# Storing the first tile of a rotary-embedding kernel in two halves, with its rows 4 to 6 computed another way

## The chip, the cores and the metric

The kernel runs on one core of a Trainium2 chip. The metric is the device time of one execution in microseconds (us); smaller is better. Times before the change: 162.01, 161.99 and 161.97 us, median 161.99 us.

## The reference

```python
# x: (16, 512, 1024) float32; cos, sin: (512, 32) float32; 16 heads of 64
x = x.reshape(16, 512, 16, 64)
x1, x2 = x[..., :32], x[..., 32:]
out = concatenate([x1 * cos - x2 * sin, x1 * sin + x2 * cos], axis=-1)
```

The angle depends on the position in the sequence alone and is the same for all heads. In all, 33.55 MB are read and 33.55 MB are written.

## The kernel before

**Tiles and rows.** The 8192 sequence positions are cut into 8 tiles of 8 rows (`TILES`, L33). A "row" here is one position on each of the 128 partitions, 1024 numbers wide, so there are 64 rows, numbered u = 0 to 63; tile t holds rows 8t to 8t + 7. A tile is 4 MB (4096 KB in the profile), 32 KB on each partition. Each entry of `TILES` gives the number of rows, its place in the ring, the pieces in which it is loaded, the pieces in which it is stored, and the numbers of the stores that have to be complete before it may be loaded. Rows are computed in place: the result of a row goes back into the row's own slot of `x_sb`, a ring of 40 rows (`RING`, L43), which is five tiles. So the first five tiles are loaded at once, and tiles 5, 6 and 7 reuse the places of tiles 0, 1 and 2 once those are stored. Tile 0 is loaded in two halves, tile 7 is stored in two halves, and all the rest moves as whole tiles: nine loads of x and nine stores.

**The work of one row.** Each row takes three steps.

1. The cosine product `x * cos`, written to one of three buffers in PSUM (`t1_ps`, `NT1 = 3`). VectorE does it, in `mul` (L322, instruction L346).
2. The sine product, of x with its halves swapped and a sine table that has the signs in it, written to one of six buffers in SBUF (`t2_sb`, `NT2 = 6`). GpSimd does it, in `on_gpsimd` (L267). Where `TWO` (L74) marks a row, one instruction makes the product of that row and the next (L299, 2048 elements per partition); otherwise one instruction makes one row (L295, 1024 elements). Row 3 of each tile (`V_ROWS`, L65) is VectorE's (L334).
3. The sum of the two, back into `x_sb`. There are two ways. For most rows VectorE adds (`comb`, L353, instruction L356). For the rows marked in `PE2` (L68), that is rows 1, 3 and 5 of a tile (from row 2 on and below row 52), TensorE adds the sine product onto the cosine product in PSUM by four multiplications with the identity (L257), and ScalarE copies the result into `x_sb` (L219).

VectorE's order is written out at the end of `on_vector` (L363): `mul(u)`, then `comb(u - 1)` where that row is VectorE's. `mul(u)` waits until the buffer of row u - 3 has been emptied, by VectorE's sum or by ScalarE's copy.

**The queues.** All loads are issued from ScalarE's queue (`on_scalar`, L197): the first six at the start (two halves of tile 0, then tiles 1 to 4) together with the two small tables, and the three late ones behind fixed rows of ScalarE's own loop, by `BEHIND` (L45): tile 5 behind row 23, tile 6 behind row 33, tile 7 behind row 41. Ahead of each, ScalarE waits for the stores that the tile's entry names. All stores are issued from SyncE's queue (`on_sync`, L186), in order. Each waits (`wait_added`, L164) until all rows up to a given one have been summed, by whichever way; that row is the last row of the piece, except for the first store, which is held back by one row more (`HOLD`, L84).

Of the kernel before, what the change touches and what calls it, by code (L numbers as in the profile page):

```python
# [6 lines left out]
def bass_split_heads_rope_kernel(  # L7
# [14 lines left out]
    R1 = seq // P  # L22
# [8 lines left out]


    TILES = (  # L33
        (8, 0, (4, 4), (8,), ()),
        (8, 8, (8,), (8,), ()),
        (8, 16, (8,), (8,), ()),
        (8, 24, (8,), (8,), ()),
        (8, 32, (8,), (8,), ()),
        (8, 0, (8,), (8,), (0,)),
        (8, 8, (8,), (8,), (1,)),  # L40
        (8, 16, (8,), (4, 4), (2,)),
    )
    RING = 40  # L43

# [2 lines left out]
    NU = sum(t[0] for t in TILES)  # L47
# [3 lines left out]
    rows = [(t, r) for t in range(NT) for r in range(TILES[t][0])]  # L51
# [13 lines left out]
    V_ROWS = {8: (3,)}  # L65
    V2 = [r in V_ROWS[TILES[t][0]] for t, r in rows]

    PE2 = [2 <= u < NU - 2 * R1 - 4 and u % 8 in (1, 3, 5) for u in range(NU)]  # L68

    def count(flags):  # L70
        return [sum(flags[: u + 1]) for u in range(NU)]


    TWO = [r in (0, 4, 6) for t, r in rows]  # L74
    n_pool = count([not V2[u] and not (u and TWO[u - 1]) for u in range(NU)])
    n_pe = count(PE2)
    n_comb = count([not a for a in PE2])

# [2 lines left out]
    BANK = 512  # L81
    EH = H * HD // BANK
    LEAD = 1
    HOLD = 1  # L84

    with ExitStack() as stack:
        x_sb = stack.enter_context(nc.sbuf_tensor([P, RING, H, 2, HALF], fp32))
# [55 lines left out]
        def in_dram(flat, t, o, m):  # L143
            n = TILES[t][0]
            run = flat[first_row[t] * P:(first_row[t] + n) * P, :].rearrange("(p r) d -> p (r d)", r=n)
            return run[:, o * dim:(o + m) * dim]
# [5 lines left out]
        def in_sbuf(t, o, m):  # L152
            k = TILES[t][1] + o
            return x_sb[:, k:k + m].rearrange("p n h t d -> p (n h t d)")
# [9 lines left out]
        def wait_added(eng, u):  # L164
            if n_pe[u]:
                eng.wait_ge(sem_a, n_pe[u])
            if n_comb[u]:
                eng.wait_ge(sem_v, n_comb[u])

        def wait_t2_free(eng, u):  # L170
            if u >= NT2:
                v = u - NT2
                if PE2[v]:
                    eng.wait_ge(sem_e, n_pe[v])
                else:
                    eng.wait_ge(sem_v, n_comb[v])
# [5 lines left out]
        def wait_landed(eng, t, r):  # L182
            if (t, r) in load_at:
                eng.wait_ge(sem_in[load_at[t, r]], 16)

        def on_sync(sp):  # L186
            for u in range(NU):
                if u not in store_after:
                    continue
                k = store_after[u]  # L190
                t, o, m = stores[k]

                wait_added(sp, u + HOLD if k == 0 else u)
                sp.dma_start(in_dram(of, t, o, m), in_sbuf(t, o, m)).then_inc(sem_out.get(k, sem_rest), 16)
            sp.wait_ge(sem_rest, 16 * (len(stores) - len(awaited)))

        def on_scalar(ae):  # L197
# [18 lines left out]
            for u in range(NU):  # L216
                if PE2[u]:
                    ae.wait_ge(sem_e, n_pe[u])
# [7 lines left out]
        def on_tensor(pe):  # L226
# [22 lines left out]
            for u in range(NU):  # L249
                if not PE2[u]:  # L250
                    continue
# [15 lines left out]
        def on_gpsimd(pl):  # L267
# [12 lines left out]
            for u in range(NU):  # L280
                t, r = rows[u]
                n = TILES[t][0]
                wait_landed(pl, t, r)
                if V2[u] or (u and TWO[u - 1]):
                    continue
                if n not in seen:
                    seen.add(n)
                    pl.wait_ge(sem_s, SIZES.index(n) + 1)
                m = 2 if TWO[u] else 1
                for v in range(u, u + m):  # L290
                    if v == u + m - 1 or PE2[v - NT2] != PE2[v + 1 - NT2]:
                        wait_t2_free(pl, v)
# [15 lines left out]
        def on_vector(ve):  # L308
# [54 lines left out]
            for u in range(NU + LEAD):  # L363
                if u < NU:
                    mul(u)
                if u >= LEAD and not PE2[u - LEAD]:
                    comb(u - LEAD)

        on_sync(nc.sync)
        on_scalar(nc.scalar)  # L370
        on_gpsimd(nc.gpsimd)
# [35 lines left out]
```

## Time and profile before

| | us |
|---|---|
| median of three runs | 161.99 |
| the profiled execution | 161.94 |
| its span, first to last instruction | 160.5 |
| outside the span (161.94 - 160.5) | 1.44 |

| engine | busy us | share of the span |
|---|---|---|
| VectorE (DVE) | 133.9 | 83% |
| GpSimd (POOL) | 127.0 | 79% |
| TensorE (PE) | 62.5 | 39% |
| ScalarE (ACT) | 21.8 | 14% |

The DMA moved 67.25 MB, 419 GB/s over the span. The page gives busy shares for the whole span and in 40 slices. The last of the profile's parts used here is the trace's list of DMA packets, with start, duration, size and queue of each: queue q10 is ScalarE's (the loads), q1 is SyncE's (the stores). Each piece is cut into 128 packets, one for each partition, eight for each of 16 DMA engines: 32 KB each for a piece of eight rows, 16 KB each for one of four.

The moments of the transfers in the profiled execution, in us from the start of the span:

| transfer | issued | first packet | landed |
|---|---|---|---|
| load of tile 4 | 4.28 | 46.98 | 66.55 |
| load of tile 5 | 60.69 | 66.34 | 85.90 |
| load of tile 6 | 86.67 | 90.27 | 110.86 |
| load of tile 7 | 103.02 | 109.72 | 130.32 |
| store of tile 0 | 35.56 | 39.90 | 60.60 |
| store of tile 1 | 49.65 | 59.27 | 79.95 |
| store of tile 2 | 65.47 | 78.64 | 94.50 |
| store of tile 7, first half | 144.22 | 148.87 | 155.61 |
| store of tile 7, second half | 152.13 | 153.78 | 160.45 |

### The profile page before, as it was taken

What the parts mean: (1) busy time and instruction counts of PE and PEld (TensorE: products, weight loads), DVE (VectorE), ACT (ScalarE), POOL (GpSimd) and SP (SyncE); (2) the same over time, 40 slices, a digit from 0 to 9 for tenths busy, and PEclk for the clock granted to TensorE, in tenths of its full rate; (3) what the DMA queues carried; (4) which work ended last, traced back from release to release, by engine and by line L of the source; (5) the groups of instructions that cost most, each with busy time, mean ns of one, the idle gap of its engine ahead of it and who ended that gap; (6) DMA issues with size and microseconds to landing.
All of it is one profiled execution on the core that took longest, in us unless ns stands there. A gap on an engine that the chain in (4) does not pass through costs nothing.

```text
span 160.5 us, 488 instructions
## 1 busy us (share of the span) xinstructions
PE 62.5 (39%) x90; PEld 22.0 (14%) x90; DVE 133.9 (83%) x120; ACT 21.8 (14%) x23; POOL 127.0 (79%) x38
## 2 busy tenths in 40 slices
PE   6050039048923761489038922893174000000000
PEld 1040023022302220223022301230121000000000
DVE  0023898999899999999999899999999977999800
ACT  0410002202220222022202220213022000000000
POOL 1009999999999999999998999883999559994000
PEclk9999999965585799557965597559569655555555
DMA  5999999999999999999999999999999999999995
GB/s 155 419 439 457 433 482 392 392 515 351 433 392 466 449 392 459 449 400 408 498 400 400 506 392 408 490 408 408 425 466 400 433 457 417 417 449 441 392 421 249
DMA packets 2882, 67.25 MB, mean 419 GB/s; under 512 B 321, under 2 KB 577, under 8 KB 577
## 3 DMA queue, kind: packets, MB, share of 16 engines
q10 hardware_dynamic: 1584, 33.69, 49.8%
q1 hardware_dynamic: 1296, 33.56, 48.5%
q14 instruction: 2, 0.01, 0.0%
HBM read 33.69 MB, written 33.55 MB: 419 GB/s over the span
## 4 chain that ended last, share of the span: by engine, by line
DVE 34%; DMA 21%; issue 15%; PE 13%; POOL 7%; ACT 3%; ACTq 1%; DVEq 0%; POOLq 0%
DMA x_sb<-in_x_dram 17%; DVE x_sb L356 16%; DVE t_ps L346 15%; PE t_ps L257 12%; POOL t_sb L299 6%; DMA stage<-in_sin_dram 4%; DVE t_sb L334 3%; ACT x_sb L219 3%; POOL t_sb L295 1%; PE tab_ps L240 1%; PE t_ps L240 1%; ACTq L203 0%; ACT sine L214 0%; ACTq L180 0%; ACT sine L215 0%
## 5 line engine op out<-in xcount | busy, mean ns | idle before, releaser
L299 POOL TENSOR_TENSOR t_sb<-x_sb,sine 128x2048 f32<-128x2048 f32 x24 | 108.2, 4530 | 18.5 <-ACT sine L215 10.5
L346 DVE TENSOR_TENSOR t_ps<-x_sb,tab_ps 128x1024 f32<-128x1024 f32 x64 | 76.9, 1222 | 13.1 <-PE t_ps L240 9.9
L257 PE MATMUL t_ps<-t_sb,ident 128*128 128x512 f32 x76 | 57.7, 915 | 53.5 <-DVE t_ps L346 47.5
L356 DVE TENSOR_TENSOR x_sb<-t_ps,t_sb 128x1024 f32<-128x1024 f32 x45 | 54.7, 1217 | 4.2 <-POOL t_sb L299 4.1
L257 PEld LDWEIGHTS t_ps<-t_sb,ident 128*128 128x128 f32 x76 | 19.6, 284 | 91.1 <-DVE t_ps L346 74.7
L219 ACT ACTIVATE x_sb<-t_ps 128x1024 f32<-128x1024 f32 x19 | 19.5, 1024 | 92.1 <-PE t_ps L257 92.1
L295 POOL TENSOR_TENSOR t_sb<-x_sb,sine 128x1024 f32<-128x1024 f32 x8 | 18.9, 2359 | 0.0
L334 DVE TENSOR_TENSOR t_sb<-x_sb,tab_ps 128x1024 f32<-128x1024 f32 x8 | 9.7, 1212 | 0.0
L230 PE MATMUL t_ps<-zero 128*128 128x512 bf16 x6 | 2.7, 627 | 1.3 <-DVE zero L309 1.3
L240 PE MATMUL tab_ps<-stage,chosen 128*128 128x128 f32 x4 | 1.2, 453 | 5.0 <-DMA stage<-in_sin_dram 5.0
L207 ACT ACT_TABLE_LOAD x1 | 1.3, 1283 | 4.8 <-issue 4.8
L240 PEld LDWEIGHTS tab_ps<-stage,chosen 128*128 128x128 f32 x4 | 0.9, 321 | 5.8 <-issue 5.8
L240 PE MATMUL t_ps<-stage,chosen 128*128 128x128 f32 x4 | 1.1, 421 | 0.0
L230 PEld LDWEIGHTS t_ps<-zero 128*128 128x128 bf16 x6 | 0.7, 135 | 2.4 <-DVE zero L309 1.2
L309 DVE MEMSET zero<- 128x256 uint32 x1 | 0.3, 272 | 0.9 <-PEq L389 0.9
L214 ACT ACTIVATE sine<-t_ps 128x256 f32<-128x256 f32 x1 | 0.4, 384 | 4.5 <-PE t_ps L240 4.5
L240 PEld LDWEIGHTS t_ps<-stage,chosen 128*128 128x128 f32 x4 | 1.0, 333 | 0.0
L268 POOL MEMSET ident<- 128x128 f32 x1 | 0.2, 206 | 0.3 <-POOLq L389 0.3
L207 ACT ACTIVATE chosen<-ident 128x256 f32<-128x256 f32 x1 | 0.4, 429 | 0.0
L215 ACT ACTIVATE sine<-t_ps 128x256 f32<-128x256 f32 x1 | 0.4, 378 | 0.0
L270 POOL TENSOR_SCALAR_AFFINE_SELECT ident<-ident 128x128 f32<-128x128 f32 x1 | 0.3, 295 | 0.1
L389 POOL MEMSET const-float32-0.0<- 128x1 f32 x1 | 0.1, 99 | 0.3 <-issue 0.3
(5 smaller groups left out, 0.7 us busy)
## 6 DMA issues: line engine op xcount, KB each, us to landing
x_sb<-in_x_dram ACTq DMA_DIRECT2D x7, 4096.0 KB, 27.3
out_dram<-x_sb SPq DMA_DIRECT2D x7, 4096.0 KB, 29.0
x_sb<-in_x_dram ACTq DMA_DIRECT2D x2, 2048.0 KB, 9.4
out_dram<-x_sb SPq DMA_DIRECT2D x2, 2048.0 KB, 9.9
stage<-in_cos_dram ACTq DMA_DIRECT2D x1, 64.0 KB, 7.3
stage<-in_sin_dram ACTq DMA_DIRECT2D x1, 64.0 KB, 7.0
```

The costliest lines, as they stand in the source:

```text
L207: ae.activation(pick[n][:], ident[:].rearrange("q (s k) -> q k s", k=m)[:, :, None, :].broadcast_to([P, m, m, P // m]), COPY,).then_inc(se ...
L214: ae.activation(s_sb[n][:, :, 0, :], raw_sin[n], COPY, scale=-1.0)
L215: ae.activation(s_sb[n][:, :, 1, :], raw_sin[n], COPY).then_inc(sem_s, 1)
L219: ae.activation(xs[:, place_of(u), :], t1_ps[:, u % NT1, :], COPY).then_inc(sem_a, 1)
L230: pe.matmul(t1_ps[:, k, b * BANK:(b + 1) * BANK], zero[:, 0:P], zero[:], start=True, stop=True).then_inc(sem_w, 1)
L240: ins = pe.matmul(to[:, k * R1:(k + 1) * R1, :].rearrange("p r d -> p (r d)"), pick[n][:, k].rearrange("q b s -> q (b s)"), stage[:, c, :] ...
L257: ins = pe.matmul(t1_ps[:, u % NT1, b * BANK:(b + 1) * BANK], ident[:], t2[:, b * BANK:(b + 1) * BANK], start=False, stop=True, skip_group ...
L295: pl.tensor_tensor(t2_sb[:, u % NT2, :, :, :], swapped(k), over_heads(s_sb[n][:, r]), mult).then_inc(sem_p, 1)
L299: pl.tensor_tensor(t2_sb[:, u % NT2:u % NT2 + 2].rearrange("p n h t d -> p (n h) t d"), x_sb[:, k:k + 2, :, ::-1, :].rearrange("p n h t d ...
L334: ve.tensor_tensor(t2_sb[:, u % NT2, :, :, :], swapped(k), over_heads(v_ps[n][:, V_ROWS[n].index(r)]), mult,)
L346: ve.tensor_tensor(t1_ps[:, u % NT1, :].rearrange("p (h d) -> p h d", d=HALF), x_sb[:, k, :, :, :].rearrange("p h t d -> p (h t) d"), c_ps ...
L356: ve.tensor_tensor(xs[:, place_of(u), :], t1_ps[:, u % NT1, :], t2_sb[:, u % NT2, :, :, :].rearrange("p h t d -> p (h t d)"), add,).then_i ...
```

## The change

Tile 0 is stored as two pieces of four rows. The first is issued when row 5 has been summed (row 3, the last of the piece, and two more), the second when row 10 has been summed (row 7 and three more). Since there is one store more, the numbers in the last column of `TILES` move: the load of tile 5 waits for both halves of tile 0. In tile 0 alone, the sine products of rows 4 and 5 become two single instructions instead of one for both, row 5 is summed by VectorE instead of TensorE and ScalarE, and row 6 by TensorE and ScalarE instead of VectorE.

```diff
     TILES = (
-        (8, 0, (4, 4), (8,), ()),
+        (8, 0, (4, 4), (4, 4), ()),
...
-        (8, 0, (8,), (8,), (0,)),
-        (8, 8, (8,), (8,), (1,)),
-        (8, 16, (8,), (4, 4), (2,)),
+        (8, 0, (8,), (8,), (0, 1)),
+        (8, 8, (8,), (8,), (2,)),
+        (8, 16, (8,), (4, 4), (3,)),
     )
...
-    PE2 = [2 <= u < NU - 2 * R1 - 4 and u % 8 in (1, 3, 5) for u in range(NU)]
+    PE2 = [2 <= u < NU - 2 * R1 - 4 and u % 8 in ((1, 3, 6) if u < 8 else (1, 3, 5)) for u in range(NU)]
...
-    TWO = [r in (0, 4, 6) for t, r in rows]
+    TWO = [r in (0, 4, 6) and (t, r) != (0, 4) for t, r in rows]
...
-    HOLD = 1
+    HOLD = {0: 2, 1: 3}
...
-                wait_added(sp, u + HOLD if k == 0 else u)
+                wait_added(sp, u + HOLD.get(k, 0))
```

## The prediction

> **What bounds the kernel now.** I read the page's slices first: no engine is full, but the DMA row is.
>
> ```profile
> DMA  5999999999999999999999999999999999999995
> GB/s 155 419 439 457 433 482 392 392 515 351 433 392 466 449 392 459 449 400 408 498 400 400 506 392 408 490 408 408 425 466 400 433 457 417 417 449 441 392 421 249
> ```
>
> Only the first and the last of 40 slices are not full. The queues say what fills it: loads and stores, half each.
>
> ```profile
> q10 hardware_dynamic: 1584, 33.69, 49.8%
> q1 hardware_dynamic: 1296, 33.56, 48.5%
> ```
>
> The two GB/s extremes in the second row are packets counted where they start, so I summed the packet records with each packet spread over its duration. That gives 433 GB/s in nearly every 2 us stretch from 4 to 158 us, for loads alone, stores alone or both, with two holes: 335 GB/s in 38 to 40 us, and 412 GB/s in 112 to 116. The floor follows: 67.25 MB at 433 GB/s are 155.3 us, and the first packet starts at 1.80, so a kernel that keeps this stream full cannot end its packets before 157.1; they end between 158.6 and 160.13. Moving transfers about inside a full stream gains nothing by itself.
>
> Next the chain of work that ended last, to see whether compute could matter too:
>
> ```profile
> 103.01 0.01 ACT x_sb L219
> 103.02 27.31 DMA x_sb<-in_x_dram
> 130.32 0.07 issue
> 130.39 4.52 POOL t_sb L299
> ...
> 149.81 2.25 DVE x_sb L356 x2
> ```
>
> ScalarE's row 41 releases the load of tile 7, this lands at 130.32, and tile 7's eight rows take until 152.06. The waits of SyncE's queue close it:
>
> ```profile
> SPq L168 <- DVE x_sb L356: 148.1, 9, 34.7
> SPq L195 <- DMA out_dram<-x_sb: 8.0, 1, 8.0
> ```
>
> The last store is issued at 152.13 and needs 8 us. Its first packet starts only at 153.78, each engine going on from the half before it without a gap: the DMA still has a backlog when compute is done. Of its 16 landings, 14 lie at 158.91 to 159.53, the two others at 160.15 and 160.45. **The end is one late DMA engine.** Its lateness is old. The packet records show a load packet at 38.24 that took 2.68 us where 1.21 is usual, just ahead of the first store's first packets; the other 15 took 1.47 to 1.85 there. At 62.08 a store packet took 1.56, beside an 8 KB instruction fetch (61.78, 0.31 us), and the second late engine appears in the landings after that.
>
> **The change part by part.** *The sine products.* The pair of rows 4 and 5 took 4.50 us start to start (13.49 / 3, L299); a single one takes 2.31 (16.30 to 18.61, L295). Two are 4.62: GpSimd is 0.12 us later from row 6 on. Rows 4 and 5 would be ready at 20.97 and 23.28 instead of 23.11 both. VectorE's order decides when they are used:
>
> ```profile
> 25.84 1.22 DVE L356 TENSOR_TENSOR x_sb<-t_ps,t_sb 128x1024 f32<-128x1024 f32 x1
> 27.47 2.36 DVE L346 TENSOR_TENSOR t_ps<-x_sb,tab_ps 128x1024 f32<-128x1024 f32 x2 [0.41 <-ACT x_sb L219]
> 29.74 1.22 DVE L356 TENSOR_TENSOR x_sb<-t_ps,t_sb 128x1024 f32<-128x1024 f32 x1
> ```
>
> Row 4 is summed at 25.84, so both cases are early, and row 8's product, at 32.10 + 0.12, is used at 34.26. Cost: nothing, covered by 2 us.
>
> *The sums.* VectorE has as many as before. Its order after 27.47 becomes product 6, sum 5, product 7, product 8, instead of product 6, product 7, sum 6, product 8: with 1.13 us from start to start, row 5 is summed at 28.60 to 29.82, and product 8 still starts at 30.87. New is that product 9 (33.13) needs row 6 from TensorE and ScalarE. TensorE can start at 28.74 (product 6 ends 28.70). Four multiplications took 3.78 us for row 3 (22.59 to 26.37) and 1.98 for row 5 (26.39 to 28.37, at a granted clock of 0.98 in the window 26 to 34). With ScalarE's 1.02 and two handovers of 0.04 row 6 is in place at 31.8 or 33.6: product 9 waits 0 or 0.5 us. I take 0, from the nearer row, whose clock window covers it, with 0.5 as the upper end. Below zero: if the clock stays high until row 11, the wait of 0.41 us (ACT, ahead of product 14) goes, so compute moves by -0.4 to +0.5. The Trainium skill's page "TensorE: Matmul & The Clock Gate", section "Part 1: The HAM clock gate", has the array fall back to half clock after an idle window of about 3.4 us; the gap ahead of row 6 would be 28.74 - 26.37 = 2.37 us, so by it the wait is 0 and the +0.5 case goes.
>
> *The stores.* The first half is issued at 29.82 + 0.08 = 29.9 instead of 35.56, the second behind row 10's sum (38.79 + 1.22) at 40.1. One issue more is 0.33 us on SyncE, which waits 148 us anyway. With the first store's own delay (35.56 to 39.90, 4.34 us) the first packet runs at 34.2. From 40 to 59 us a load packet and a store packet alternate on each engine: the store's 8 packets took 59.07 - 39.90 = 19.2 us, 2.40 each, two times 1.21. Half-tile packets take 0.61, so a round is 1.82 us, loads get two thirds, and the first half needs 8 x 1.82 = 14.6 us, to 48.8; the second follows with no gap, since it is issued at 40.1. Tiles 3 and 4 have about 14.5 load packets per engine left at 34.2, that is 26.4 us, so they are in at about 61 (before: 65). The second half ends at 62 and lands at 62 to 63.6; if shares went by bytes, it would be 34.2 + 4.19 MB / 216 GB/s = 53.6. This new wait gates the load of tile 5, issued at 60.69 before. Behind ScalarE's wait stands its copy of row 25 (70.40), 6.8 us later, so VectorE isn't reached. The load's first packet would start 3.6 us after the issue (as 86.67 to 90.27), at 64.3 to 67.2, against 66.34 before, with stores filling the gap; tile 5 lands at 86.8 at the latest and is first used at 91.27. Tiles 6 and 7 are released by ScalarE's rows 33 and 41 (86.67, 103.02), with 79.95 and 94.50 as the store landings needed, so the order of transfers is the old one from there.
>
> *The bytes.* 256 packets of 16 KB take 0.611 each instead of 128 of 1.213: 256 x 0.611 - 128 x 1.213 = 1.15 us over 16 engines, +0.07 us. The hole at the first store (15 packets lost 0.26 to 0.63, one 1.47) moves to about 33 us; I cost the move at nothing, since loads run alone around it as before. Bounds: it may vanish (-0.45 us mean, -0.92 at the late engine) or come again at the second half (+0.45).
>
> Sum against the profiled execution: 161.94 + 0.07 + 0 = 162.01; the median stands 0.05 above it: **162.05 us**. What compute moves by is hidden: the bulk of the engines has some 0.3 to 0.6 us to spare at the last store (152.13 plus 1.0 to 1.3, as the first load's 0.80 to 1.80 and 2.10, against 153.7), the late engine one more.
>
> **The rivals.** *Slower, the late engine gets later.* The place is the first store's first packet. For: one engine lost 1.47 there, and each engine's fate differs. If the engine that meets the instruction fetch is the one that is late, 160.15 - 159.53 = 0.62 is added: 162.7; if it loses a packet of 1.21 more in the new alternation, 163.2. It decides from a loss over 1.47 + 0.3. 0.16.
>
> *Slower, the second half pays again*: a hole like the first (+0.45, 162.5), up to an issue-to-packet time on idle engines (+1.0, 163.0). Against: the second half is queued 8 us before the first is done, and the last two halves landed 4.84 us apart, 2.10 MB at 433 GB/s, so a queued transfer costs nothing extra. 0.07. The Trainium skill's page "DMA: Bandwidth & Descriptors", section "Anatomy of one DMA — SWDGE (gpsimd) path", puts about 2.0 us of fixed cost on each DMA; by it, unhidden, the time would be 164.0, and the 4.84 us speak against it here.
>
> *Slower, compute*: product 9's 0.5 us passes through rows 33 and 41 to tile 7 and the last store, where it outlives the reserve: 162.4. 0.05.
>
> *Faster, the lateness does not arise.* Loads around the first store are in another phase, and only one engine in 16 was unlucky. If the second late engine stays, the end is 0.30 earlier: 162.05 - 0.30 = 161.75, 0.12. If it goes too, 0.92: 161.15; between these 0.20. Compute allows it, since tile 7's landing was itself late by that engine (129.2 for the others, and VectorE had waited 1.14).
>
> *That nothing hinges on the change*, the forecast, holds the remaining 0.40.
>
> **How the numbers follow.** A difference over 0.2%, 0.32 us, is what a measurement can tell. Same: 0.40 + 0.12 = 0.52. Faster: 0.20. Slower: 0.16 + 0.07 + 0.05 = 0.28. The range from 161.2 to 162.8 leaves out the worst of the late-engine case and a double hole.
>
> **What would show it.** Right: a DMA row of 9s, the first half issued near 29.9 and the second near 40.1, tile 5's load issued at 62 to 64, row 6's copy ended before 33.13, tile 7 landed within 1 us of 130.32, and one or two late landings at the end. Wrong: a slice with the DMA below 9 in the middle, a second group of long packets near 49, VectorE waiting for ScalarE ahead of 33.1, or all 16 last landings together.

## The result and the profile after

The changed kernel took 163.20 us (median of six runs, 162.47 to 163.34) against 161.98: ratio 1.0072, 95% interval 1.0052 to 1.0093. Two later repeats of it gave 1.0100 (1.0083 to 1.0117) and 1.0081 (1.0050 to 1.0111). It is slower, by 1.2 to 1.6 us; the prediction said 162.05, with 162.8 at most. The profiled execution took 163.32 us, 1.38 more than the one before, with a span of 161.8. Runs over 1.5% longer than the fastest of their kernel are left out of all ratios here: three of the eleven of e4 below, one of the twelve of h1 (166.20) and one of the kernel before (164.41).

The page of the changed kernel, slices and queues:

```profile
DMA  5999999989999999999899999999999999999993
GB/s 190 417 422 429 502 405 389 502 377 401 413 454 441 441 401 452 364 494 397 356 437 470 397 437 462 397 462 437 397 462 437 397 462 437 397 462 409 421 425 170
...
q10 hardware_dynamic: 1584, 33.69, 49.4%
q1 hardware_dynamic: 1440, 33.56, 48.4%
```

The row is as full as before. Two slices show an 8 (32 to 36 and 77 to 81 us), and 144 packets more are on the store queue. The chain that ended last, and SyncE's last wait:

```profile
102.03 0.01 ACT x_sb L219
102.04 27.26 DMA x_sb<-in_x_dram
129.30 0.07 issue
129.37 4.52 POOL t_sb L299
...
148.78 2.26 DVE x_sb L356 x2
```

```profile
SPq L195 <- DMA out_dram<-x_sb: 10.3, 1, 10.3
```

Compute is a microsecond **earlier** than before: tile 7 lands at 129.30 (130.32), the last sum ends at 151.04 (152.06). Yet SyncE waits 10.3 us for the last store instead of 8.0. The 16 landings of that store, one for each DMA engine, from the trace:

```
before 158.91 158.94 159.00 159.00 159.07 159.09 159.30 159.32 159.37 159.38 159.46 159.46 159.47 159.53 160.15 160.45
after  159.06 159.08 159.11 159.19 159.21 159.25 159.35 159.37 159.41 159.60 159.97 160.86 161.37 161.50 161.60 161.79
```

The middle of the row is unchanged, 159.35 and 159.39. What moved is its end: one or two late engines became five, and the last is 1.34 us later, nearly the whole difference of the profiled executions (1.38).

Where these five fell behind is in the packet records. Five store packets at 66.33 to 66.87 took 2.1 to 2.5 us instead of 1.21, just ahead of the first packet of tile 5's load (67.23); at 76.15 to 76.90 five load packets took 2.1 to 2.55, and nine more at 78.5 to 78.9 took 0.2 to 0.4 too long. From 64 to 80 us packets took 15.0 us longer than usual in sum, 0.94 us for each of 16 engines; in the profile before nothing there took longer. These are two places, not one. Ahead of the restart of the loads stand 5.4 of the 15.0 us; 9.4 are in load packets from 76 on, where the store queue goes from tile 1's store to tile 2's (no store packet starts between 75.69 and 77.33). The records have no engine numbers, but a packet starts where the one before it on its engine ended; followed in this way, the five long store packets and the five long load packets lie on the same five engines. The DMA view of that window, before and then after:

```profile
DMA packets 247, 7.05 MB, mean 440 GB/s; under 512 B 32, under 2 KB 32, under 8 KB 32
```

```profile
DMA packets 217, 6.59 MB, mean 412 GB/s; under 512 B 16, under 2 KB 16, under 8 KB 16
```

0.46 MB less in the same 16 us are 1.06 us at 433 GB/s (packets are counted where they start, so half a megabyte is also the most that the edges can hide). The view alone does not decide: the repeat e5 below, with the loss, has 7.01 MB in this window, and f3, without it, 6.82. The sum over packets is the better measure. I call the first place, the long store packets just ahead of the restart, the **restart loss** below.

The compute side did what its waits were worked out to do (VectorE, ScalarE, and ScalarE's queue of the changed kernel):

```profile
28.48 1.22 DVE L356 TENSOR_TENSOR x_sb<-t_ps,t_sb 128x1024 f32<-128x1024 f32 x1
29.61 2.35 DVE L346 TENSOR_TENSOR t_ps<-x_sb,tab_ps 128x1024 f32<-128x1024 f32 x2
31.87 1.22 DVE L356 TENSOR_TENSOR x_sb<-t_ps,t_sb 128x1024 f32<-128x1024 f32 x1
33.00 1.22 DVE L346 TENSOR_TENSOR t_ps<-x_sb,tab_ps 128x1024 f32<-128x1024 f32 x1
```

```profile
31.34 1.02 ACT L219 ACTIVATE x_sb<-t_ps 128x1024 f32<-128x1024 f32 x1 [4.04 <-PE t_ps L257]
```

```profile
63.14 0.33 ACTq L180 DMA_DIRECT2D x_sb<-in_x_dram  x1
```

Row 5 is summed at 28.48, row 6 is copied by 32.36, and product 9 starts at 33.00 with no wait. The last line is tile 5's load, issued at 63.14 as soon as the second half has landed (63.06), 2.45 us later than before.

### The profile page after: what moved, and what is told of

Read it like the earlier page. It is cut to its first block, busy times and chain, and to the rows that moved or that the text cites. A ratio compares the mean times of both kernels' runs of the same rounds, so it can differ in the third digit from the quotient of the medians.

```text
span 161.8 us, 493 instructions
## 1 busy us (share of the span) xinstructions
PE 58.9 (36%) x90; PEld 20.4 (13%) x90; DVE 133.7 (83%) x120; ACT 21.8 (13%) x23; POOL 127.1 (79%) x39
## 4 chain that ended last, share of the span: by engine, by line
DVE 36%; DMA 21%; issue 15%; PE 10%; POOL 7%; ACT 2%; ACTq 1%; DVEq 0%; POOLq 0%
DVE x_sb L356 17%; DMA x_sb<-in_x_dram 17%; DVE t_ps L346 16%; PE t_ps L257 9%; POOL t_sb L299 6%; DMA stage<-in_sin_dram 4%; DVE t_sb L334 3%; ACT x_sb L219 2%; POOL t_sb L295 1%; PE tab_ps L240 1%; PE t_ps L240 1%; ACTq L203 0%; ACT sine L214 0%; ACTq L180 0%; ACT sine L215 0%
## 5 line engine op out<-in xcount | busy, mean ns | idle before, releaser
L299 POOL TENSOR_TENSOR t_sb<-x_sb,sine 128x2048 f32<-128x2048 f32 x23 | 103.6, 4520 | 17.4 <-ACT sine L215 10.3
L257 PE MATMUL t_ps<-t_sb,ident 128*128 128x512 f32 x76 | 54.1, 857 | 56.2 <-DVE t_ps L346 50.1
L257 PEld LDWEIGHTS t_ps<-t_sb,ident 128*128 128x128 f32 x76 | 17.9, 261 | 91.9 <-DVE t_ps L346 77.3
L295 POOL TENSOR_TENSOR t_sb<-x_sb,sine 128x1024 f32<-128x1024 f32 x10 | 23.4, 2349 | 0.0
```

The costliest lines, as they stand in the source:

```text
L257: ins = pe.matmul(t1_ps[:, u % NT1, b * BANK:(b + 1) * BANK], ident[:], t2[:, b * BANK:(b + 1) * BANK], start=False, stop=True, skip_group ...
L295: pl.tensor_tensor(t2_sb[:, u % NT2, :, :, :], swapped(k), over_heads(s_sb[n][:, r]), mult).then_inc(sem_p, 1)
L299: pl.tensor_tensor(t2_sb[:, u % NT2:u % NT2 + 2].rearrange("p n h t d -> p (n h) t d"), x_sb[:, k:k + 2, :, ::-1, :].rearrange("p n h t d ...
```

## The experiments

Runs of one and the same kernel differ: the kernel before took 161.2 to 162.5 us in nearly all of its runs beside the experiments, with medians of 161.72 to 161.92. Each ratio is against those on the same chip.

The first theory was the **dry queue**: half-size store packets leave the loads two thirds of the DMA, so these run out at 61.3; the next load waits for the second half, and its restart among stores loses time. The rivals: the compute part; the earlier store; chance.

**e1, the split alone.** `PE2` and `TWO` as before.

```diff
-    PE2 = [... u % 8 in ((1, 3, 6) if u < 8 else (1, 3, 5)) ...]
+    PE2 = [... u % 8 in (1, 3, 5) ...]
-    TWO = [r in (0, 4, 6) and (t, r) != (0, 4) for t, r in rows]
+    TWO = [r in (0, 4, 6) for t, r in rows]
```

> The store in two halves alone: sine products and sums of tile 0 as before. Dry-queue theory (the second half's landing at 63.1 gates tile 5's load at 63.14, loads run out at 61.3, and at the restart near 66.5 five DMA engines lose 1.1 us each, which ends the kernel late): 163.0 to 163.4 us, several last landings over 1 us behind the bulk. Compute theory (rows 4 to 6 make it slower): 162.0.

162.49, ratio 1.0042 (1.0016 to 1.0068). Of ten runs seven lie at 161.83 to 162.53 and three at 163.22 to 163.30. The profiled one (161.83) has no restart loss, but it is the fastest of the ten. So the split costs something by itself, and by the medians less than the change (the two intervals overlap).

**e2, the compute part alone**, in the kernel before: the two lines of e1 the other way round.

> The new sine products and sums of rows 4 to 6 alone, tile 0 stored whole as before. Dry-queue theory: 161.9 to 162.1, one or two late landings at the end as before. Compute theory: 163.0 or more. Chance theory (any shift of timing redraws which DMA engines are late): anywhere between 161.2 and 163.2.

161.99, 1.0012 (0.9991 to 1.0033): not to be told from nothing. The compute theory falls, as far as these rows alone go.

**e3, both halves late.**

```diff
-    HOLD = {0: 2, 1: 3}
+    HOLD = {0: 5, 1: 1}
```

> Both halves issued behind row 8, when the whole store was issued before (about 35.5), the rest as in the changed kernel. By packets of 16 KB the loads still get two thirds and run out at about 58, the second half lands at about 62, and tile 5's load restarts an empty queue near 66. Dry-queue theory: 162.7 to 163.3, late engines from about 66. Early-start theory (it is the earlier first store that costs): 162.0 as before.

162.40, 1.0023 (1.0004 to 1.0042). The loads ran out at 58.3 and restarted at 66.8 as expected, and no packet near 66 was long. The dry queue alone does not make the loss.

**e4, tile 5 in two loads.**

```diff
-        (8, 0, (8,), (8,), (0, 1)),
+        (8, 0, (4, 4), (8,), (0, 1)),
-    BEHIND = {6: 23, 7: 33, 8: 41}
+    BEHIND = {6: 19, 7: 23, 8: 33, 9: 41}
...
-                        for j in TILES[loads[i][0]][4]:
+                        t, o, m = loads[i]
+                        n_in = len(TILES[t][2])
+                        for j in TILES[t][4] if n_in == 1 else (TILES[t][4][o // m],):
```

> The changed kernel with tile 5 loaded in two halves, each behind the store of the half whose place it takes: the first is issued at about 57 behind ScalarE's row 19, so the load queue does not run dry at 61. Dry-queue theory: 162.0 to 162.2, no group of long packets near 66. Early-start theory: 163.2 as the changed kernel.

Median 163.60, ratio 1.0081 (1.0046 to 1.0117), with a wide spread, 161.74 to 166.23. In the profiled execution, the longest of them and one of those left out of the ratio, tile 5's 16 KB load packets took turns with 32 KB store packets: its last ones ran past 92 us, where tile 5's loading had ended at 84.2 before, tile 7's last packet ended at 135.3 instead of 129.9, and the last store was issued only at 158.66. There the loads got the smaller share, which is another cause; whether the usual runs show it too isn't known, so this kernel says nothing on the theory.

**e5, the changed kernel again**, on the chip of e6 to e8.

> The changed kernel once more, beside the next three on the same chip, since the split alone came out 0.57 us over the kernel before there and the whole change 1.2 us elsewhere. If the change is the split and nothing else, 162.4 to 162.6 as the split alone; if the compute part adds to it, 163.0 or more.

163.37, 1.0100 (1.0083 to 1.0117), with the restart loss (four packets over 0.9 us too long near 66).

**e6, a dry restart without a split**: the kernel before, with tile 5's load held to row 23's sum.

```diff
                     if BEHIND[i] == u:
+                        if i == 6:
+                            ae.wait_ge(sem_v, n_comb[23])
```

> The kernel before, with tile 5's load held on ScalarE until VectorE has summed row 23 (about 65.5 instead of 60.7), so that the load queue runs dry at 65 and restarts near 69 among stores; the store of tile 0 is whole. Dry-queue theory: 162.4 to 163.2, long packets near 68. Packet-size theory (16 KB store packets taking turns with 32 KB load packets give the loads two thirds and pull the 16 DMA engines apart): 161.9 as before.

161.80, 1.0005 (0.9984 to 1.0025). The loads ran out at 64.8 and restarted at 69.0, at no cost. With e3, the dry-queue theory in its plain form is down.

**e7, two transfers of 64 partitions each**, 32 KB packets, in the kernel before.

```diff
-                sp.dma_start(in_dram(of, t, o, m), in_sbuf(t, o, m)).then_inc(sem_out.get(k, sem_rest), 16)
+                for h in ((0, 64), (64, 128)) if k == 0 else ((0, 128),):
+                    sp.dma_start(
+                        in_dram(of, t, o, m)[h[0]:h[1], :], in_sbuf(t, o, m)[h[0]:h[1], :]
+                    ).then_inc(sem_out.get(k, sem_rest), 16)
...
-                            ae.wait_ge(sem_out[j], 16)
+                            ae.wait_ge(sem_out[j], 32 if j == 0 else 16)
```

> The kernel before, with tile 0's store in two transfers of 64 partitions each, issued one behind the other behind row 8: two transfers, yet packets of 32 KB. Packet-size and dry-queue theories: 161.9 as before, loads and stores half and half. Theory of a cost for each transfer: 162.4.

166.12, 1.0295 (1.0237 to 1.0354). None of the theories had this. Packets of both queues were long from 44.9 to 65.2, where these pieces ran. A transfer of half the partitions is a thing of its own here, so it prices nothing of the change.

**e8, one store in 16 KB packets**, in the kernel before.

```diff
-                sp.dma_start(in_dram(of, t, o, m), in_sbuf(t, o, m)).then_inc(sem_out.get(k, sem_rest), 16)
+                to, frm = in_dram(of, t, o, m), in_sbuf(t, o, m)
+                if k == 0:
+                    to = to.rearrange("p (a d) -> p a d", a=2)[:, ::-1, :]
+                    frm = frm.rearrange("p (a d) -> p a d", a=2)[:, ::-1, :]
+                sp.dma_start(to, frm).then_inc(sem_out.get(k, sem_rest), 16)
```

> The kernel before, with tile 0's store as one transfer issued behind row 8, cut into 16 KB packets by naming the two halves of each partition in the other order. Packet-size theory: 162.4 as the split ones, loads out at about 58. Theory of a cost for each transfer, or of the earlier start: 161.9.

161.91, 1.0008 (0.9990 to 1.0025), although the loads ran out at 59.2 and restarted at 66.6. Packet size and dry queue together cost nothing measurable.

So neither part of the change was expensive alone, nor the packets. What was left was the **moment**: e1 issues its first half at 29.14, the change at 29.78, since row 5 is summed by VectorE. In the profile after, engines part there: the first half lands at 47.6 to 47.9 on eleven engines and at 48.5 to 49.0 on five. I supposed that the border between two load pieces near 32.2 does it.

**f1, the split alone at the change's moment.**

```diff
                 wait_added(sp, u + HOLD.get(k, 0))
+                if k == 0:
+                    sp.wait_ge(sem_m, 8)
```

> The split alone, with sums and sine products as before, but SyncE waits in addition for product 7, so that the first half is issued at about 29.85 as in the changed kernel, and not at 29.14. Phase theory (0.6 us later, the store's first packets meet the engines at the border of two load pieces near 32.2; some engines take their first store packet one turn later than the others, and lose over 1 us more near 66): 163.2 to 163.4. Compute theory (rows 4 to 6 themselves add 0.9): 162.4 to 162.5 as the split alone.

162.73, 1.0064 (1.0039 to 1.0090), restart loss in the profile. In this profile the moment brings the loss without the compute part. The time lies between the two theories' figures, and its interval overlaps that of e1, so the times alone do not tell the two moments apart.

**f2 and f3, the change with its first half later and earlier**: `HOLD = {0: 3, 1: 3}` and `HOLD = {0: 1, 1: 3}`.

> The changed kernel with the first half held back by three rows instead of two: issued at about 32.4, first packets near 36.3, in the middle of tile 3's load. Phase theory: 162.3 to 162.6. Compute theory, and a plain cost of two halves with early start: 163.2 to 163.4.

> The changed kernel with the first half held back by one row: issued at about 27.4, first packets near 31.4, ahead of the border. Phase theory: 162.3 to 162.6 if 31.4 is clear of the border, else as the change. Compute theory: 163.2 to 163.4. Theory that the earlier the first store, the more is lost: 163.5 or more.

f2, issued at 33.60: 162.20, 1.0025 (1.0006 to 1.0045). f3, issued at 27.44: 162.01, 1.0011 (0.9994 to 1.0029), so no loss that can be measured with an even earlier store. Compute part, split and early start are all in f3: none of them is the cost by being there.

**f4, the change with the restart held to row 23's sum** (the lines of e6).

> The changed kernel, with tile 5's load held on ScalarE until VectorE has summed row 23 (about 65.4 instead of 63.3). If the loss near 66 belongs to the moment of this restart: 162.3 to 162.6, or long packets moved to near 69. If the engines were parted at the first store already and lose at whatever moment the load queue restarts: 163.2 to 163.4, with long packets near 69.

162.69, 1.0080 (1.0048 to 1.0112). The long store packets went along with the restart: six at 68.7 to 69.0, ahead of the load's first packet at 69.19. The loss belongs to the restart, not to its clock time.

**g1, the change a third time; g2, no border; g3, a moment between.** g2 loads tiles 2 and 3 as one transfer; g3 waits for product 8 (`sp.wait_ge(sem_m, 9)`).

```diff
             t, o, m = loads[i]
-            eng.dma_start(in_sbuf(t, o, m), in_dram(xf, t, o, m)).then_inc(sem_in[i], 16)
+            if t == 3:
+                return
+            to, frm = in_sbuf(t, o, m), in_dram(xf, t, o, m)
+            if t == 2:
+                to = x_sb[:, TILES[2][1]:TILES[2][1] + 16].rearrange("p (a n) h t d -> p a (n h t d)", a=2)
+                frm = xf[first_row[2] * P:first_row[4] * P, :].rearrange("(a p r) d -> p a (r d)", a=2, r=8)
+            eng.dma_start(to, frm).then_inc(sem_in[i], 16)
...
-                eng.wait_ge(sem_in[load_at[t, r]], 16)
+                eng.wait_ge(sem_in[load_at[2 if t == 3 else t, r]], 16)
```

> The changed kernel a third time, as the measure for the next three on the same chip: 163.0 to 163.4, long store packets near 66.

> The changed kernel with tiles 2 and 3 loaded as one transfer, so that the border of two load pieces near 32.2, just where the first store packets come in, is gone; the first half is still issued at about 29.8. Border theory (the loss needs the first store to meet a border): 162.0 to 162.5, no long store packets near 66. If only the moment of the issue counts, or the restart of the load queue: 163.0 to 163.4.

> The changed kernel with the first half issued only when product 8 is done, at about 32.15, between the 29.8 of the change and the 33.6 that gave 162.2: its first packets come in near 36, clear of the border at 32.2. Border theory: 162.0 to 162.4. If 33.6 was better for another reason, between 162.4 and 163.4.

g1: 163.24, 1.0081 (1.0050 to 1.0111). The change has now come out slower in all three of its measurements, each time with long packets near 66 in the profile, so chance falls as a rival too. g2: 163.37, 1.0104 (1.0073 to 1.0136), the engines part and lose as in the change. Tile 2's rows now wait for both tiles, and the last store is issued at 153.14 instead of 151.12; the median of its landings is 159.37 all the same. **The border theory is down.** g3, issued at 32.16: 162.47, 1.0049 (1.0030 to 1.0069), without the restart loss; just over the border theory's figure.

**g4, the whole store, held back by two rows, with the restart held.** `HOLD = 2` in the kernel before, and the lines of e6.

> The kernel before with its whole store of tile 0 held back by two rows (issued at about 39.3, which stands to the border of the loads of tiles 3 and 4 at 41.7 as 29.8 stands to 32.2), and tile 5's load held to row 23's sum, so that the load queue restarts empty. If a border at the first store and a restart are enough, with 32 KB packets too: 162.4 to 163.2, long store packets near 69. If it needs the half-size packets or the two pieces: 161.8.

163.17, 1.0092 (1.0071 to 1.0113). A restart loss with no split at all, on all engines (median of the last landings 160.67). The DMA view of 64 to 80 us for it:

```profile
DMA packets 207, 6.26 MB, mean 391 GB/s; under 512 B 16, under 2 KB 16, under 8 KB 16
```

Now what do the kernels with the loss have in common? In each, tile 4's load and the last store of tile 0 land together. Two runs were to break and to make that meeting: **h1** keeps the change's first moment and holds the second half to row 15 (`HOLD = {0: 2, 1: 8}`); **h2** takes f3's first moment and issues the second half later (`HOLD = {0: 1, 1: 5}` and a wait for TensorE's row 13).

> The changed kernel with its first half issued as there (29.8), but the second held back to row 15 (about 49.6), so that the loads run alone from 47.5 to 53: tile 4 lands at about 59.2, the second half still at about 62.3. Theory of the meeting (the loss comes when tile 4's load and tile 0's last store land within half a microsecond of each other, 62.0 and 62.3 in the change, which all nine kernels with a loss or without fit so far): 162.0 to 162.5, no long store packets near 66. Theory of the first moment (29.8 is enough): 163.0 to 163.4.

> The kernel whose first half is issued at 27.4, which took 162.01 (tile 4 in at 64.9, second half at 60.1), with the second half issued at about 44.9 instead of 40.5, so that both land near 62.2 to 62.9. Theory of the meeting: 162.8 to 163.4, long store packets near 66. Theory of the first moment: 161.9 to 162.2.

h1: 162.25, 1.0031 (1.0011 to 1.0052), eleven runs from 161.60 to 163.00 and one at 166.20, no long packet near 66:

```profile
DMA packets 238, 7.27 MB, mean 455 GB/s; under 512 B 16, under 2 KB 16, under 8 KB 16
```

The first moment is not enough. h2: 162.03, 1.0019 (1.0001 to 1.0038), where the theory of the meeting had 162.8 to 163.4. Its profile has no long packet either, though the two landed 0.2 us apart; but this execution (161.63) is the fastest of the twelve, and two others took 162.81 and 162.86. In most runs, then, the meeting is not enough by itself.

All of these side by side (e4 and e7, with causes of their own, left out); moments from the profiled executions, "in" is the median of the 16 landings, and the two columns of packets give the us in sum by which packets started in that window took longer than usual (1.21 us for 32 KB, 0.61 for 16 KB):

| kernel | first store issued | tile 4 in | tile 0's last store in | store packets, 64 to 72 | load packets, 72 to 82 | ratio |
|---|---|---|---|---|---|---|
| before | 35.56 | 65.82 | 58.53 | 0.0 | 0.0 | 1 |
| e2 compute alone | 35.61 | 65.97 | 58.66 | 0.0 | 0.0 | 1.0012 |
| e6 late restart | 35.49 | 65.73 | 58.48 | 0.1 | 1.4 | 1.0005 |
| f3 earlier | 27.44 | 64.86 | 60.10 | 0.0 | 0.0 | 1.0011 |
| e8 16 KB packets | 35.51 | 59.42 | 62.40 | 0.0 | 2.8 | 1.0008 |
| e3 halves late | 35.50 | 59.16 | 62.17 | 0.0 | 0.0 | 1.0023 |
| f2 later | 33.60 | 59.89 | 62.31 | 0.0 | 10.3 | 1.0025 |
| h1 second half late | 29.73 | 59.05 | 62.15 | 0.0 | 0.2 | 1.0031 |
| g3 between | 32.16 | 60.87 | 62.27 | 0.3 | 2.0 | 1.0049 |
| h2 made to meet | 27.34 | 62.58 | 62.78 | 0.0 | 0.0 | 1.0019 |
| e1 split alone | 29.14 | 61.97 | 62.16 | 0.0 | 0.6 | 1.0042 |
| f1 split, at 29.9 | 29.92 | 61.81 | 62.24 | 4.0 | 12.6 | 1.0064 |
| f4 change, late restart | 29.85 | 62.11 | 62.31 | 5.8 | 8.3 | 1.0080 |
| the change | 29.78 | 62.02 | 62.27 | 5.4 | 9.4 | 1.0072 |
| e5 the change | 29.75 | 62.08 | 62.34 | 5.1 | 1.2 | 1.0100 |
| g1 the change | 29.70 | 62.07 | 62.33 | 6.9 | 4.9 | 1.0081 |
| g2 no border | 29.67 | 62.11 | 62.35 | 9.4 | 6.5 | 1.0104 |
| g4 whole, late | 39.05 | 62.03 | 62.22 | 7.8 | 13.3 | 1.0092 |

**What is shown:** of these, seven kernels have a restart loss in their profile, 4.0 us or more in the store packets of 64 to 72 us, and all others 0.3 or less. Each of the seven costs at least 0.6%, every other one less than 0.5%, though neighbours' intervals overlap and each kernel has one profile. The loss comes just ahead of the restart of the load queue and moves with it (f4); all seven profiles with it have the two landings within 0.5 us; and in h1, with the meeting taken away, it is gone. To take it away h1 issues the second half 10 us later, so the meeting is not the only thing that differs.

**What is argued only:** how much of the time is the restart loss and how much the second place. For the restart speaks e5, with 5.1 us there, 1.2 at the second place and the ratio 1.0100. But f2's profiled execution, the longest of its twelve (162.84), lost 10.3 us in load packets at the second place, with nothing at the restart and the landings 2.4 us apart. So the second place may have a price of its own, and the meeting is no condition for it.

**What stays open:** why some engines lose a packet's time there, and why h2, and most runs of e1, meet without losing. That engines part at the first half is not the condition: in h2 its landings lie at 45.4 to 45.7 on ten engines and 46.7 to 47.0 on six, without a loss, and in g4 nothing has parted ahead of the loss (tile 3's load lands within 0.34 us). The slow runs of e1 and h2 have no profile. The trace has no record of what an engine does inside a long packet. Open too is the smaller cost of a split without the restart loss, 0.1 to 0.5% (f3, h2, e3, f2, h1, e1, g3), of the size of the spread between runs.

## Why the prediction was wrong

*The bound* held: the stream of the DMA is full but for the two slices at 8, which the prediction had named as a sign of being wrong, and compute was hidden. Compute moved a microsecond earlier, outside the -0.4 to +0.5 us given for it, and this changed nothing.

*The sine products and sums* held: cost nothing in e2, row 6 copied at 32.36 of the 33.13 allowed, product 9 without a wait. The way to the copy was half right. TensorE took row 6 at 28.62 after 2.38 us idle with a first multiplication of 0.70 us, where row 3's first took 1.22. But the granted clock, 1.00 from 26.4 to 29.7, was 0.50 from 29.8 to 32.0, so it fell while the third of the four ran. They took 2.68 us in all, between the 1.98 and 3.78 of the two rows that the prediction chose from; the wait was 0 because the copy still ended 0.64 us ahead of product 9 (33.00), not because the clock stayed up.

*The moments of the stores* held: issued at 29.78 and 39.97 (29.9 and 40.1), loads out at 61.3 (61), the second half in at 63.06 (62 to 63.6), tile 5's load issued at 63.14 with its first packet at 67.23 (up to 67.2). Shares went by packets: in 36 to 46 us loads moved 279 to 300 GB/s and stores 133 to 154. The rule for it is in the Trainium skill, page "DMA: Bandwidth & Descriptors", section "Queues, rings and completion order": an engine takes turns between queues packet by packet. The trace agrees.

*The step that failed* is the one on this restart: "The load's first packet would start 3.6 us after the issue", "with stores filling the gap", and behind it "the order of transfers is the old one from there". The order was; but the sum has no term for the restart itself: I costed it at nothing, as that of tile 6's load at 90.27 had been free. The runs showed 5.4 us lost there, about 1.1 on each of five engines, and about as much again on the same five at the change from tile 1's store to tile 2's, ten microseconds later, for which the sum has no term either. Five engines are 1.5 to 2.4 us behind the median at the end, which comes 1.34 us later for it. Why they lose it stays open, as said above. A row of before could have bounded one such loss: its one long packet at a queue's start cost an engine 1.47 us.

*The hole at the first store* was no worse: packets there took 6.7 us too long in sum, 8.1 before. So the rival "the late engine gets later" named the right kind of end (unequal engines, 162.7 to 163.2) and the wrong place, and I gave it 0.16 and let the range end at 162.8. That its 163.2 is also the measured time is luck. *The second half pays again* did not happen: all packets of 46 to 56 us together took 0.5 us too long. The fixed cost of about 2.0 us for each DMA, which the Trainium skill's page "DMA: Bandwidth & Descriptors" states in its section "Anatomy of one DMA — SWDGE (gpsimd) path", is a fit for transfers issued from GpSimd; these are issued from SyncE, and no run here tests it. What a transfer more costs here, f3 shows: it has the extra one and a ratio of 1.0011, 0.2 us.

## What to carry to other kernels

In a kernel whose DMA stream is full, the mean busy share can't tell two versions apart: look at the landings of the last transfer engine by engine, and trace the late ones back to the packets that took too long. Treat a queue that runs empty and starts again beside another one as a place that may have a price (here between nothing and 1.7 us of 162), which sub-microsecond shifts elsewhere can switch on. A change that only shifts such moments is worth measuring in several placements (here 27.4 to 39.1) before its idea is judged.

## What was not expected of the hardware

- The restart loss: packets of 1.21 us that took 2.1 to 2.5 on five of 16 engines, again on the same five ten microseconds later, and lateness that is kept to the end of the kernel. In the last five stores of the change (130 to 162 us) the latest engine stays the same 2.4 us behind the median.
- A store in two transfers of 64 partitions cost 4.3 us (e7), with 32 KB packets and the same bytes.
- The same program spreads by over a microsecond from run to run (161.2 to 162.5 before), and by more where the restart is near its edge: e1 has a group at 162.4 and one at 163.2.
